# A macaron decoder trunk on eight cores: equal tile-major stages, half of an FFN's weights resident, all engines ordered by a list scheduler, input and output without transposes

## The chip, the cores and the metric

One Trainium2 chip, all eight NeuronCores. Two dies of four cores each: cores 0 to 3 and 4 to 7. Every core runs the same program on its own tokens; the cores do not talk to each other. The metric is the device time of one execution in microseconds (us), that of the slowest core.

A run can fall into a slow state: the cores of one die, or of both, show a lower granted TensorE clock, and their spans are longer (at 0.813 on one die, beside 0.996 to 0.998 in the fast runs). "Limiter" below is a name for whatever lowers the clock; what sets it off is not shown here. Every comparison below is either between fast runs or between dies on which the clock was left alone. Such a die is called undisturbed.

## The reference

Four layers; each is FFN, token mixer, FFN, each with a norm before and after it. Layers 0 and 2 mix with a gated convolution of width 3, layers 1 and 3 with causal pooling over 2, 4, 8 or 16 positions.

```python
def rmsnorm(x, g):
    y = x * lax.rsqrt(jnp.mean(x * x, axis=-1, keepdims=True) + EPS)
    return y * g
def swiglu(h, w_gate, w_up, w_down):
    return (silu(h @ w_gate) * (h @ w_up)) @ w_down
for i in range(4):                                   # D_MODEL 1024, D_FF 2816
    x = x + 0.5 * rmsnorm(swiglu(rmsnorm(x, g[0]), ...), g[1])
    h = rmsnorm(x, g[2])
    m = conv_mixer(h, ...) if i % 2 == 0 else pool_mixer(h, ...)
    x = x + rmsnorm(m, g[3])
    x = x + 0.5 * rmsnorm(swiglu(rmsnorm(x, g[4]), ...), g[5])
# ... outputs: y for 8 x 2048 prompt and 128 x 4 sample tokens, and the mixers' last rows
```

A core has 2,112 tokens. It does them in two passes of 1,056, each held on the chip as three tiles of 352 tokens. Activations lie feature-major: 8 chunks of 128 features on the partitions, tokens along the free dimension. All products are in bf16 with fp32 sums, so every matmul is 128 x 128 by 128 x 352.

## The kernel before

An operation list with hand-placed interleaving. Each engine is given its instructions in the order in which the program recorded them; semaphores are derived from the keys read and written. A tile's norms are recorded "deferred" and drained a few at a time between the matmuls of what follows.

```python
GROUPS = [5, 5, 4, 4, 4]        # FFN chunks of 128 hidden features; RING = 10 weight slots
def ffn(base_idx, finish, need, groups=GROUPS, prefix=1):
    units = [(gi, t) for t in range(NTILE) for gi in range(prefix)]
    units += [(gi, t) for gi in range(prefix, len(groups)) for t in range(NTILE)]
    # AB(ui): gate and up products of a unit, silu on ACT, product on DVE into gt
    # OUT(ui): for c in range(8): G matmuls into pso; ACT copies (gi == 0) or DVE adds into acc
    yield from AB(0)
    for ui in range(1, len(units)):
        yield from AB(ui)
        yield from OUT(ui - 1)          # finish(t) after the last group: the norms of tile t
# ...
def norm_stats(src, skey, t):           # ACT squares; 8 matmuls with ones sum them into pss (PSUM)
    # ...                               # ACT: Ln and Exp, in place in pss
def postnorm(l, n, t, half):            # DVE: acc = acc * gain * pss; x += acc on POOL (5) and DVE (3)
# ...
def pool_mixer(l, p, base_idx, finish, need):
    for t in range(NTILE):
        yield ("need", need(t))         # the pre-norm of the tile must be done
        for g in range(4):
            # per chunk: copy to a work tile, log2(w) shifted adds on POOL or DVE,
            # DVE: b2 = window / w - u; then 2 x 2 matmuls and a scale by DVE
        finish(t)
def boundary(p_store, p_load):          # between the passes, and at both ends
    # rows of 128 tokens: DMA to staging, 8 transposes on PE, ACT copies to xT; and back for y
```

Everything is recorded through one helper, so the profile names one line for it all; instructions are told apart by their tiles: psa are gate and up products, pso the down and mixer products, pss the sums of squares, b the bf16 squares (or mixer inputs), hreg the normed input, mt the mixers' scratch.

## Time and profile before

| | before |
|---|---|
| median of the first 3 runs | 5,863.55 us (5,766.8 to 6,026.48) |
| spans by core, profiled run | 5,696 to 5,888 us |
| PE busy, slowest core | 84% |
| fast runs on all chips used | 5,740 to 5,777 us, one of 5,804 us |

From the page of the profiled execution (the slowest core, core 1). First the span, then busy time and share of each engine, then the span in 40 slices: busy tenths of PE, and the clock granted to PE in tenths; then groups of instructions with their count, busy us, mean ns, and the engine's idle time just before them.

```profile
span 5887.5 us, 76218 instructions; the slowest of 8 cores (5696.2 to 5887.5 us)
...
PE 4964.6 (84%) x30208; PEld 3064.3 (52%) x30208; DVE 2439.9 (41%) x4900; ACT 1937.9 (33%) x3961; POOL 722.5 (12%) x1188
...
PE   6989999939988989975979789996698978989398
...
PEclk7777787858999999987989899997799989999599
...
L172 PE MATMUL psa<-hreg,ring 128*128 128x352 bf16 x18432 | 2991.1, 325 | 168.8 <-DMA ring<-wstream 94.5
...
L172 DVE TENSOR_TENSOR acc<-pso,acc 128x352 f32<-128x352 f32 x1536 | 791.7, 523 | 224.2 <-PE pso L172 179.2
...
L172 PE MATMUL pss<-b,ones_bf 128*128 128x352 bf16 x1152 | 273.1, 397 | 211.2 <-ACT b L172 81.5
```

PE is busy 84% and dips at four places, the four pool mixers (two layers in two passes). The 18,432 and 1,152 matmuls shown, 8,448 down products and two smaller groups of the page (960 and 768) make 29,760 of 352 columns, the work that no ordering removes.

Core 0 and core 2 of the same execution and die, in the same 200 us; the columns are the stretch, busy time and count of PE, weight loads, DVE, ACT and POOL, then the clock, the DMA share and GB/s:

```profile
600.00:800.00 200.00, 193.40 (x1051) 113.06 (x1049) 63.86 (x127) 44.27 (x82) 10.93 (x17) 0.80 0.26 48
```

```profile
600.00:800.00 200.00, 187.57 (x1240) 119.73 (x1238) 85.14 (x170) 61.05 (x119) 18.14 (x28) 1.00 0.43 80
```

Both are dense, but core 0 is granted 0.80 of the clock and gets 1,051 matmuls through, core 2 1.00 and 1,240. So core 1, which the page shows, is not the one to cost the change from. Core 4 was hardly limited and spans 5,696 us. Its waits of PE (us in total, times, longest):

```profile
PE pso L172 <- DVE b L172: 307.2, 44, 15.2
PE pso L172 <- DVE acc L172: 170.3, 116, 5.2
PE pss L172 <- ACT b L172: 86.4, 52, 4.5
...
PE psa L172 <- DMA ring<-wstream: 65.8, 25, 4.5
```

And five stretches of 20 us around its first pool mixer, columns as above:

```profile
1000.00:1020.00 20.00, 20.00 (x136) 13.12 (x135) 6.83 (x13) 9.69 (x18) 0.00 (x0) 1.00 0.31 63
1020.00:1040.00 20.00, 13.90 (x78) 7.23 (x76) 15.19 (x33) 13.07 (x29) 5.60 (x8) 0.91 0.00 0
1060.00:1080.00 20.00, 5.06 (x16) 2.07 (x16) 14.02 (x32) 5.84 (x16) 6.72 (x11) 0.50 0.68 141
...
1140.00:1160.00 20.00, 3.88 (x12) 1.48 (x12) 14.35 (x24) 6.67 (x20) 12.71 (x22) 0.50 0.00 0
1180.00:1200.00 20.00, 17.44 (x116) 11.08 (x115) 8.23 (x18) 15.72 (x29) 4.53 (x5) 1.00 0.00 1
```

136 matmul records per 20 us is full speed; in the middle of the mixer it is 12 to 26, and the clock is about 0.5 where PE idles: on core 4 it was 0.50 to 0.64 in 28 of the 32 such windows in which PE was busy for under 10 us, and 0.996 on the mean of the 134 in which PE never paused. DVE, ACT and POOL are not full either: it is one chain, each step waiting for the one before. Adding up what every 20 us window of core 4 falls short of 136 gives 1,175 us, of which about 480 at the four pool mixers.

### The profile page before, as it was taken

What the parts mean: (1) busy time and instruction counts of PE and PEld (TensorE: products, weight loads), DVE (VectorE), ACT (ScalarE), POOL (GpSimd) and SP (SyncE); (2) the same over time, 40 slices, a digit from 0 to 9 for tenths busy, and PEclk for the clock granted to TensorE, in tenths of its full rate; (3) what the DMA queues carried; (4) which work ended last, traced back from release to release, by engine and by line L of the source; (5) the groups of instructions that cost most, each with busy time, mean ns of one, the idle gap of its engine ahead of it and who ended that gap; (6) DMA issues with size and microseconds to landing.
All of it is one profiled execution on the core that took longest, in us unless ns stands there. A gap on an engine that the chain in (4) does not pass through costs nothing.

```text
span 5887.5 us, 76218 instructions; the slowest of 8 cores (5696.2 to 5887.5 us)
## 1 busy us (share of the span) xinstructions
PE 4964.6 (84%) x30208; PEld 3064.3 (52%) x30208; DVE 2439.9 (41%) x4900; ACT 1937.9 (33%) x3961; POOL 722.5 (12%) x1188
## 2 busy tenths in 40 slices
PE   6989999939988989975979789996698978989398
PEld 4545555615655556542646455553365644656155
DVE  1244333363434534355332543435434363343634
ACT  2133323134232433324141343423514135151342
POOL 0011001030101101013010110102201011010401
PEclk7777787858999999987989899997799989999599
DMA  4333222311333314230332332332032431414121
GB/s 85 70 55 60 38 54 45 74 34 30 68 70 70 66 38 81 49 70 17 70 97 49 70 66 40 79 60 60 8 74 45 92 65 29 90 29 92 34 49 47
DMA packets 64230, 341.58 MB, mean 58 GB/s; under 512 B 7390, under 2 KB 7646, under 8 KB 63840
## 3 DMA queue, kind: packets, MB, share of 16 engines
q0 software_dynamic: 57600, 314.60, 28.3%
q1 hardware_dynamic: 6272, 22.10, 1.1%
q8 instruction: 238, 3.90, 0.3%
q14 instruction: 120, 0.98, 0.1%
HBM read 641.66 MB, written 11.02 MB: 111 GB/s over the span
## 4 chain that ended last, share of the span: by engine, by line
PE 70%; DVE 10%; ACT 8%; DMA 5%; issue 4%; POOL 3%; ACTq 0%; POOLq 0%; SPq 0%; DVEq 0%
PE psa L172 44%; PE pso L172 23%; DVE acc L172 5%; PE pss L172 4%; DMA ring<-wstream 4%; ACT L172 3%; DVE hreg L172 2%; ACT b L172 2%; POOL xT L172 2%; DVE mt L172 1%; ACT pss L172 1%; POOL mt L172 1%; DVE b L172 1%; POOL ring L172 1%; ACT sa L172 1%
## 5 line engine op out<-in xcount | busy, mean ns | idle before, releaser
L172 PE MATMUL psa<-hreg,ring 128*128 128x352 bf16 x18432 | 2991.1, 325 | 168.8 <-DMA ring<-wstream 94.5
L172 PEld LDWEIGHTS psa<-hreg,ring 128*128 128x128 bf16 x18432 | 1860.5, 101 | 1244.7 <-DMA ring<-wstream 72.5
L172 DVE TENSOR_TENSOR gt<-psa,sa 128x352 bf16<-128x352 f32 x1056 | 553.7, 524 | 2452.2 <-PE psa L172 2059.2
L172 PE MATMUL pso<-gt,ring 128*128 128x352 bf16 x8448 | 1424.8, 327 | 147.0 <-DVE acc L172 140.2
L172 ACT ACTIVATE sa<-psa 128x352 f32<-128x352 f32 x1056 | 488.1, 464 | 2573.3 <-PE psa L172 2546.1
L172 PEld LDWEIGHTS pso<-gt,ring 128*128 128x128 bf16 x8448 | 842.1, 101 | 684.5 <-DVE acc L172 208.7
L172 DVE TENSOR_TENSOR acc<-pso,acc 128x352 f32<-128x352 f32 x1536 | 791.7, 523 | 224.2 <-PE pso L172 179.2
L172 POOL DMA_DIRECT2D ring<-wstream x400 | 214.0, 554 | 2881.6 <-PE pso L172 2834.0
L172 POOL TENSOR_TENSOR xT<-xT,acc 128x352 f32<-128x352 f32 x360 | 333.4, 953 | 1616.0 <-DVE acc L172 1505.4
L172 PE MATMUL pss<-b,ones_bf 128*128 128x352 bf16 x1152 | 273.1, 397 | 211.2 <-ACT b L172 81.5
L172 PE MATMUL pso<-b,ring 128*128 128x352 bf16 x960 | 186.9, 356 | 311.4 <-DVE b L172 307.0
L172 ACT ACT_TABLE_LOAD x297 | 381.1, 1283 | 140.9 <-PE psa L172 135.6
L172 DVE SCALAR_TENSOR_TENSOR hreg<-xT,params_sb,pss 128x352 bf16<-128x352 f32 x480 | 245.3, 575 | 240.3 <-ACT pss L172 240.3
L172 ACT ACTIVATE b<-xT 128x352 bf16<-128x352 f32 x576 | 259.1, 490 | 164.5 <-POOL xT L172 116.9
L172 PEld LDWEIGHTS pss<-b,ones_bf 128*128 128x128 bf16 x1152 | 129.7, 118 | 338.0 <-issue 72.4
L172 PEld LDWEIGHTS pso<-b,ring 128*128 128x128 bf16 x960 | 98.0, 107 | 396.1 <-DVE b L172 316.3
L172 ACT ACTIVATE acc<-pso 128x352 f32<-128x352 f32 x480 | 222.7, 464 | 220.2 <-PE pso L172 219.4
L172 ACT ACTIVATE b<-acc 128x352 bf16<-128x352 f32 x576 | 238.9, 487 | 15.2 <-DVE acc L172 15.2
L172 DVE SCALAR_TENSOR_TENSOR acc<-acc,params_h,pss 128x352 f32<-128x352 f32 x384 | 200.2, 575 | 78.4 <-ACT pss L172 78.4
L172 DVE SCALAR_TENSOR_TENSOR mt<-mt,params_sb 128x352 f32<-128x352 f32 (+2 forms) x256 | 126.4, 494 | 88.8 <-ACT mt L172 84.3
L172 ACT ACTIVATE pss<-pss,epst 128x352 f32<-128x352 f32 x144 | 76.0, 528 | 247.0 <-PE pss L172 246.5
L172 DVE SCALAR_TENSOR_TENSOR acc<-acc,params_sb,pss 128x352 f32<-128x352 f32 x192 | 101.0, 575 | 115.8 <-ACT pss L172 115.8
(56 smaller groups left out, 1369.1 us busy)
## 6 DMA issues: line engine op xcount, KB each, us to landing
ring<-wstream POOLq DMA_DIRECT2D x400, 768.0 KB, 12.6
mt<-x_in SPq DMA_DIRECT2D x16, 512.0 KB, 7.7
y_o<-mt SPq DMA_DIRECT2D x16, 512.0 KB, 3.2
stg<-spool SPq DMA_DIRECT2D x4, 480.0 KB
ps_s<-spool SPq DMA_DIRECT2D x4, 352.0 KB
ps_s<-stg SPq DMA_DIRECT2D x32, 16.0 KB
mt<-x_in SPq DMA_DIRECT2D x2, 128.0 KB, 3.1
stg<-sconv SPq DMA_DIRECT2D x4, 64.0 KB
```

The costliest lines, as they stand in the source:

```text
L172: ins = attr(*a, **k)
```

## The change

The intent: keep PE fed through every norm and mixer. Stages go tile by tile with equal work; an FFN runs in two halves of 11 chunks whose weights stay resident for all three tiles, so that two whole tiles of matmuls (78 us) lie between a tile's last product and its next need; a list scheduler with durations for every operation places all instructions of all engines at build time; tokens come in and go out feature-major, so PE transposes nothing (the host rearranges them before and after, outside the device time). The diff replaces most of the file; its core:

```diff
-GROUPS = [5, 5, 4, 4, 4]
-RING = 10
+GRP = 11
+RU = 24                     # weight ring, units of 1,024 columns: 11 gate/up pairs and one spare
+LAT = {"pe": 0.22, "act": 0.10, "dve": 0.10, "pool": 0.12, "sp": 0.05}
+MM = 0.1490
+def c_act(n, sb=False): return 0.172 + 0.000833 * n + (0.022 if sb else 0.0)
+def c_dve(n): return 0.150 + 0.001042 * n
 # ...
+class Sched:
+    def op(self, eng, fns, cost, reads=(), writes=(), vts=(), prio=0, margin=0.0, dma=None, ...):
+        # records dependencies; vts are PSUM banks, assigned when the schedule is made
+    def run(self):
+        # event-driven list scheduling: at each step the engine and operation that can start
+        # first, ties by (prio, program order); 7 banks for products, 1 for the sums of squares
+                else:
+                    t = o.end + LAT[e] + q.margin     # when a successor on another engine may start
 # ...
-        P.op("act", ... Exp, in place in pss)          # post-norm products read pss in PSUM
+        S.op("act", [Ln in place, lambda a: a.activation(out=rr[b][:], in_=B(v)[:, 0:TS], func=AF.Exp, scale=-0.5)], ...)
+            S.op("pe", f, 4 * MM, reads=[... ("sq", b, c) ...], vts=[v], prio=P_STAT, margin=0.6)
 # ...
+    def ffn(f, finish):
+        for g in range(2):
+            slots = [load_units(wab[f, g * GRP + jj], 2) for jj in range(GRP)]
+            # ... 8 loads of down weights, wdn[dc], 11 chunks each
+            for t in range(NTILE):
+                ffn_tile(g, t, slots, finish)
 # ...
+            def fin1(t, ...):
+                postnorm(l, 1, t, True)
+                prenorm(l, 2, t, to_u=not conv)
+                if not conv:
+                    pool_tile(l, p, t, fin2)            # a tile's whole pool mixer, norms included
 # ...  pool windows of 8 and 16 by one DVE scan each; conv and pool squares straight from PSUM
-    def boundary(p_store, p_load): ...                  # transposes and staging
+    def load_x(p, t): ...                               # DMA to x[t] as it lies, and store_y back
```

## The prediction

> **What bounds it now.** TensorE: the page gives PE 84% of the span, the chain of waits is 70% PE. The groups hold 29,760 real matmuls of 352 columns (18,432 + 8,448 + 960 + 768 + 1,152; 448 more are transposes). In undisturbed 20 us windows a core completes 136, 147 ns each: 29,760 x 0.147 = 4,370 us, a floor at full clock. Core 4, hardly limited, spans 5,696 us: some 1,300 us is not dense matmul.
>
> Where that lies (20 us windows of core 4, PE's waits):
> - four pool mixers, each 130-150 us with 8-29 matmuls per 20 us at clock 0.5: about 120 us lost each, 480 us. The waits name DVE b (307 us), DVE acc, ACT b: one chain of norm, windows, small matmul, norm, norm.
> - first 80 us: about 50 lost; pass boundary and end (transposes, staging): about 80.
> - conv mixers, FFN seams, ring waits (66-95 us), each 3-18 us per window: the rest, about 600.
>
> **What the change does.** FFN and stats matmuls and weight bytes stay. It removes the transposes, their evictions and fences, and the pass boundary's serial store and load. Groups of 11 instead of 4-5 cut the accumulate adds (1,536 x 523 ns) to 384: 600 us less DVE, off the critical path. One FFN half x one tile is 264 matmuls, 39 us, so a tile's norm chain has the other two tiles' 78 us as cover. I estimate a post+pre-norm chain at 26 us (16 squares of 0.49, two Ln/Exp with 1.28 us table loads, 16 products of 0.575, 8 adds): hidden. Pool: about 80 us, and ACT needs about 44 us per 39 us tile: nearly hidden, 15 us left each. Weights per half are 8.65 MB; the first windows moved 150-215 GB/s, so 40-58 us of 118: hidden.
>
> **Fast state (estimate).** 4,370 + start 30 + end 25 + pools 4 x 15 + imperfect static order 1.5% (65) = 4,550 us. DVE and ACT about 40% busy, PE 96-97%.
>
> **Limiter.** Cores 0 and 1 ran at 0.81 from the start to about 1,150 us, cores 2 and 3 from about 4,450 to 5,560; others stayed at 1.00 in the same dense code. [...] dense dies ran at 1.00, and pairs were hit. An episode cost 150-200 us. [...] Held throughout it would be 29,760 x 0.177 + 200 = 5,470 us.
>
> **Prediction.** 4,700 us for the median run (best near 4,550), range 4,500 to 5,250. Faster by over 2%: 0.97, within 2%: 0.01, slower: 0.02.
>
> **Right if:** pool stages no longer dip in the slices of PE; dense windows hold 136 matmuls per 20 us at 1.00, 113 where limited; DVE b vanishes from PE's waits; table loads stay near 290; weight loads aren't among PE's waits beyond the first 100 us.
>
> **Wrong if:** the limiter holds throughout; all cores' weight bursts, concentrated in the third tile, exceed what HBM gives and PE waits at each half; weight issues on POOL, blocked on buffers, hold up residual adds; ACT or DVE saturates around the pool mixers; or the fixed order, made with modelled times, stalls in-order engines.

The fast state came to 4,550 us, and a run held at the lower clock throughout to 5,470 us. The 0.177 us in the latter is 20 us over 113 matmuls, which is the count at 0.81 (112 or 113 in the windows of cores 0 and 1 from 960 to 1,000 us, against 136 at 1.00). The point of 4,700 us lies 150 us above the fast state; that the median run would be a slow one was the author's estimate, not shown.

## The result, and the profile after

| | before | after |
|---|---|---|
| median of 6 runs | 5,820.38 us (5,750.89 to 6,289.14) | 4,808.14 us (4,533.64 to 5,433.13) |
| fast runs | 5,751 to 5,777 us | 4,533.64 and 4,534.30 us |
| ratio of the fast runs | | 0.7857 (95%: 0.7812 to 0.7902) |
| PE busy, profiled run | 84% | 98% |

A ratio is the mean time of one kernel's fast runs over that of the other's of the same rounds, so not quite the ratio of the medians quoted. Only two of the six new runs were fast; the other four had one die or both at a lower clock, from 4,708 us (0.955) to 5,433 us (0.813).

The page after, of a fast execution, the same lines as before (core 6):

```profile
span 4532.7 us, 70376 instructions; the slowest of 8 cores (4528.3 to 4532.7 us)
...
PE 4459.6 (98%) x29760; PEld 2911.6 (64%) x29760; DVE 1926.4 (42%) x3581; ACT 1832.7 (40%) x3527; POOL 824.2 (18%) x1329
...
PE   7999999999999999999999999999999999999998
...
PEclk9999999999999999999999999999999999999999
...
L350 PE MATMUL ps<-h,ring 128*128 128x352 bf16 x19200 | 2924.4, 313 | 0.0
...
L350 DVE TENSOR_TENSOR acc<-ps,acc 128x352 f32<-128x352 f32 x384 | 200.7, 523 | 454.3 <-PE ps L350 453.8
...
L350 PE MATMUL ps<-sq,ones_bf 128*128 128x352 bf16 x1152 | 223.0, 318 | 58.4 <-ACT sq L350 39.9
```

The four dips are gone from the slices. VectorE's adds fell from 1,536 to 384. PE on core 4 before was idle for 908 us and busy for 4,788 (at a mean clock of 0.914); here it is idle for 73 and busy for 4,460 (at 0.996). So most of the gain is idle time, and some 330 us are busy time, with the clock at 0.996 instead of 0.914 and the 448 transposes gone. These are all the waits of PE:

```profile
PE ps L350 <- ACT sq L350: 39.9, 23, 11.4
PE ps L350 <- ACT rr L350: 18.4, 13, 3.1
PE ps L350 <- DVE gt L350: 0.8, 2, 0.6
```

59 us in all, none of them for weights. Windows around the first pool mixer, and one long dense stretch:

```profile
840.00:860.00 20.00, 18.90 (x127) 12.21 (x126) 11.54 (x27) 13.09 (x27) 2.61 (x4) 1.00 0.16 27
880.00:900.00 20.00, 18.50 (x123) 11.75 (x122) 16.38 (x27) 10.17 (x19) 8.77 (x14) 1.00 1.04 163
920.00:940.00 20.00, 16.35 (x97) 9.68 (x95) 16.62 (x33) 16.08 (x29) 3.81 (x5) 0.91 0.00 1
940.00:960.00 20.00, 20.00 (x136) 13.11 (x134) 14.68 (x34) 10.76 (x25) 5.79 (x9) 1.00 0.08 32
1200.00:1800.00 600.00, 599.76 (x4020) 393.02 (x4019) 250.10 (x472) 234.48 (x452) 106.87 (x190) 1.00 0.46 74
```

97 to 127 records where there had been 12 to 26. By the same count core 6 falls short of full speed by 79 us, 38 of them at the pools and nearly all the rest in the first 60 us; the last 13 us, after its last matmul, come on top. The long stretch also corrects a reading: 4,020 records in 600 us are 149.3 ns each, or 149.2 by the 599.76 us for which PE was busy. A 20 us window counts the matmuls that stick out of either end too, so 136 records are about 134 matmuls.

### The profile page after: what moved, and what is told of

The parts are those of the page before. It is cut to its first block, busy times and chain, and to the rows that moved or that the text cites. A ratio compares the mean times of both kernels' runs of the same rounds, so it can differ in the third digit from the quotient of the medians.

```text
span 4532.7 us, 70376 instructions; the slowest of 8 cores (4528.3 to 4532.7 us)
## 1 busy us (share of the span) xinstructions
PE 4459.6 (98%) x29760; PEld 2911.6 (64%) x29760; DVE 1926.4 (42%) x3581; ACT 1832.7 (40%) x3527; POOL 824.2 (18%) x1329
## 4 chain that ended last, share of the span: by engine, by line
PE 93%; DVE 4%; ACT 2%; DMA 1%; issue 0%; SPq 0%; DVEq 0%
PE ps L350 93%; DVE acc L350 2%; DMA x<-x_in 1%; ACT sq L350 1%; DVE x L350 1%; DVE gt L350 0%; ACT L350 0%; DVE h L350 0%; ACT ps L350 0%; ACT sa L350 0%; ACT rr L350 0%; DVE scr L350 0%; ACT acc L350 0%; SPq L350 0%; DVEq L368 0%
## 5 line engine op out<-in xcount | busy, mean ns | idle before, releaser
L350 PE MATMUL ps<-h,ring 128*128 128x352 bf16 x19200 | 2924.4, 313 | 0.0
L350 PEld LDWEIGHTS ps<-h,ring 128*128 128x128 bf16 x19200 | 1881.4, 98 | 990.7 <-DVE h L350 0.5
L350 PE MATMUL ps<-gt,wdn 128*128 128x352 bf16 x9216 | 1406.6, 313 | 1.1 <-DVE gt L350 0.8
L350 DVE TENSOR_TENSOR gt<-ps,sa 128x352 bf16<-128x352 f32 x1056 | 550.2, 522 | 1929.7 <-PE ps L350 1893.1
L350 PEld LDWEIGHTS ps<-gt,wdn 128*128 128x128 bf16 x9216 | 901.2, 98 | 475.6 <-DVE gt L350 2.9
L350 ACT ACTIVATE sa<-ps 128x352 f32<-128x352 f32 x1152 | 531.8, 462 | 1387.6 <-PE ps L350 1333.1
L350 POOL TENSOR_TENSOR x<-x,acc 128x352 f32<-128x352 f32 x288 | 323.6, 1146 | 979.9 <-DVE acc L350 979.2
L350 ACT ACTIVATE sq<-x 128x352 bf16<-128x352 f32 x576 | 271.5, 494 | 190.5 <-DVE x L350 83.4
L350 DVE SCALAR_TENSOR_TENSOR acc<-acc,params_h,rr 128x352 f32<-128x352 f32 x384 | 312.1, 861 | 28.5 <-ACT rr L350 28.5
L350 DVE SCALAR_TENSOR_TENSOR h<-x,params_sb,rr 128x352 bf16<-128x352 f32 x480 | 254.6, 578 | 51.3 <-ACT rr L350 50.8
```

Of the source, the lines that this page charges most:

```text
L350: ins = attr(*a, **k)
```

## The experiments

The theory after the result: in the fast state the gain is PE's idle time at chains, put under the matmuls of other tiles. Rivals were that resident weights, fewer VectorE adds or the missing transposes carry it, and that the scheduler's durations hardly matter. All kernels below gave correct results. In what follows the undisturbed die's span is quoted; the new kernel's is 4,531 us, the kernel before has about 5,740 us. The first four runs were on one chip, the others on two more; the new kernel was run again on one of these as a control, and gave the same span.

### Program order on three engines

The scheduler stays, but PE, DVE and ACT must take their operations in the order of the program.

```diff
+        if eng in ("pe", "act", "dve"):
+            prev = self.prev_on.get(eng)
+            if prev is not None and prev.idx not in deps:
+                prev.succ.append(o)          # order only, no semaphore
+                o.ndep += 1
+            self.prev_on[eng] = o
```

> The new kernel, but TensorE, VectorE and ScalarE take their instructions in the order in which the program lists them; weight loads and the other work of POOL and SP stay list-scheduled. Theory A (the gain is that other tiles' matmuls are put into the time of a tile's norm chain, which the list scheduler does): every chain stands open again. 72 tiles at seams x about 15 us (3 us before each sum of squares, 12 us between the two norms) plus some 45 us for each of 12 pool tiles: a span of 5,900 to 6,600 us in the fast state, PE busy 65 to 75%, waits of PE for ACT and DVE instead of near none. Rival B (resident half weights, fewer adds and feature-major input and output carry the gain, and the order only polishes it): under 4,900 us.

Measured: all four runs had a slow die; undisturbed dies took 5,743 to 5,764 us, so at least 1,212 us more than the new kernel. Waits of PE on core 4 of the less disturbed die:

```profile
PE ps L357 <- ACT sq L357: 732.3, 216, 22.5
PE ps L357 <- DVE h L357: 173.6, 48, 8.9
```

The size was missed (5,900 or more was expected); the direction and the waits are as theory A had them. Rival B falls: with every structural part of the change in place and only the order undone, the whole gain is gone, to within some 25 us. (Program order is harsher than the order before, which was interleaved by hand; so this does not say that the structure is worth nothing, but that it gains nothing in this order.)

### Groups of 5, 5, 4, 4, 4 again

```diff
+GS = [5, 5, 4, 4, 4]
-        for g in range(2):
-            slots = [load_units(wab[f, g * GRP + jj], 2) for jj in range(GRP)]
+        for g in range(len(GS)):
+            slots = [load_units(wab[f, G0[g] + jj], 2) for jj in range(GS[g])]
# gate and up products in program order, and after the buffer they lead to is free: without it the
# scheduler stops, all PSUM banks held by products whose successors wait for a bank
```

With two groups of 11 these added order rules leave PE's order nearly as it is: the scheduler, run without a chip, gives about 40 lines of difference in 3,648 entries, and 4,506 us instead of 4,497 by its own durations. What they cost with the small groups was not separated, since the scheduler stops without the first rule.

> The new kernel with FFN groups of 5, 5, 4, 4, 4 chunks as before, instead of two halves of 11; list scheduler kept. Theory A (what counts is the cover that the last and first group give a tile's chain: two tiles of a group of 4 are 2 x 14.3 = 28.6 us, not 78): ordinary chains of about 26 us just fit, pool chains of about 80 us do not. About 80 to 100 us lost at each of four pool mixers, a few us at the other seams: 4,850 to 5,050 us in the fast state, dips of PE at the pools only. Rival B (the list scheduler does it with any group size): under 4,600 us. Rival C (the saved VectorE adds carry it, 1,536 instead of 384): loss spread evenly over the FFN stretches, not at the pools.

Measured: 4,918.16 and 4,917.17 us, both fast, 4,893 us on die 0: 362 us more. Page of that run and waits of core 0:

```profile
PE 4578.6 (93%) x29760; PEld 2933.6 (60%) x29760; DVE 2528.6 (51%) x4733; ACT 1724.1 (35%) x3453; POOL 1047.4 (21%) x1713
...
PE   7999999789999999969989999996999999999698
```

```profile
PE ps L358 <- ACT sq L358: 128.7, 43, 11.6
PE ps L358 <- DVE h L358: 84.6, 35, 9.3
```

The dips are back at the pools: by the count of windows about 285 of 439 us short of full speed lie there, against 38 of 79 in the new kernel, 62 us more at each pool mixer. Rival B falls, and rival C too: VectorE is busy 51% instead of 42%, but the loss does not follow its work. The remaining 110 us or so sit at the other seams, more than "a few us": probably an ordinary chain does not quite fit in 28.6 us. So, the added order rules apart, the resident half pays as cover, not as saved adds.

### Gates at the pool mixers, then at every seam

```diff
+    def gate():              # written when the last tile has left the stage
+        S.op("dve", lambda v: v.memset(gtile[:], 0.0), 0.1, reads=[("x", NTILE - 1, c) ...], writes=["gate"])
+            ffn(2 * l, fin1)
+            if not conv:
+                gate()
+                for t in range(NTILE):
+                    prenorm(l, 2, t, to_u=True, gated=True)    # its squares read "gate"
+                    pool_tile(l, p, t, fin2)
```

> The new kernel, but no tile enters the pool mixer before the last tile has left the FFN in front of it (four gates). Theory A (the pool's long chain is hidden because tile 0 may run it while TensorE works on tiles 1 and 2): at each gate the chain of tile 0 from the norm through the windows to the next norm, about 55 us, stands open, less the 12 us lost there now: 4,700 to 4,830 us in the fast state. Rival (the pool mixer itself has become cheap through scans and through copies from PSUM, so that its place matters little): under 4,600 us.

Measured: 4,720 us on die 0 (4,762.66 us for the run; the other die was at 0.966). 189 us more, 47 us a gate. Waits of PE there:

```profile
PE ps L350 <- ACT sq L350: 119.6, 34, 12.0
PE ps L350 <- DVE h L350: 67.9, 24, 5.8
```

Theory A, with its size; the cheaper mixer alone would have left under 70 us.

> As the one with four gates, with gates at all seams within a pass, 18 in all, so that no tile begins the next stage's norm before the last tile has left the stage before. Theory A: 14 more gates of about 20 to 26 us each on top of the four at the pools, 280 to 360 us more than that run: about 5,050 to 5,200 us in the fast state. Rival (the ordinary seams are hidden by something else, such as weight prefetch): less than 100 us more than the run with four gates.

Measured: 5,037 to 5,040 us on die 0 (5,059.82 us for the fast run), 318 us more than with four gates, 23 us for each of the 14 others. As expected for theory A. ("Every seam" leaves out the one behind each pool mixer and the one between the passes, which have no gate.) The chains that lie hidden are therefore about 47 us at a pool and 23 us elsewhere. (The last tile's post-norm is within the gate, so these are upper values of what stands open.)

### Wrong durations for the scheduler

```diff
-        o.cost = cost
+        o.cost = cost if eng in ("pe", "sp") or dma else 0.5 * cost
-LAT = {"pe": 0.22, "act": 0.10, "dve": 0.10, "pool": 0.12, "sp": 0.05}
+LAT = {"pe": 0.0, "act": 0.0, "dve": 0.0, "pool": 0.0, "sp": 0.0}
-                cost += 1.35          # table load
+                cost += 0.65
```

> The new kernel, its list scheduler fed with wrong durations: everything outside TensorE and the DMA costs half of what the trace shows, and semaphore latencies count as zero. Theory A (the order is robust, because 78 us of cover is three times an ordinary chain, so durations need not be right): the span grows by less than 1%, 4,530 to 4,580 us in the fast state, the growth at the pools. Rival (the calibrated costs are what makes the order fit, and a wrong model stalls the in-order engines): over 4,650 us.

Measured: 5,067 to 5,079 us on undisturbed dies, 5,088.81 us in the one fast run: 537 us more. My theory failed here and the rival held. PE's waits, core 5:

```profile
PE ps L350 <- ACT sq L350: 334.3, 128, 11.3
PE ps L350 <- DVE h L350: 66.9, 39, 3.8
```

128 waits for squares, 2.6 us each. Cover does not help an instruction that stands too early in a fixed order: at each of these waits PE stood still at a sum of squares whose squares were late, and the gate products behind it waited too. In the trace what followed the sums went on without a pause after 123 of the 128 waits, so it had been ready. That became the next theory.

### The same wrong durations, sums of squares held back

```diff
-                 prio=P_STAT, margin=0.6)
+                 prio=P_STAT, margin=6.0)      # and the same for the pool's products
```

> The run with halved costs took 5,068 us on an undisturbed die, so the earlier theory of a robust order fell. This kernel has the same wrong costs, but the scheduler keeps every small matmul that sums squares (and the pool's matmuls) 6 us behind what feeds it, instead of 0.6 us. Theory A' (with wrong costs those matmuls stand in TensorE's fixed order before their squares exist, and TensorE, which takes matmuls in order, stands still at each; cover is of no use if the matmul is placed too early): PE's wait for ACT sq falls from 334 us to under 80 us, and the span to 4,600 to 4,750 us on an undisturbed die. Rival (everything is misplaced: gates, evictions, table switches, bank choice): the span stays above 4,900 us.

Measured: 4,801 to 4,814 us on the better die, between the two expectations. Waits of PE, core 0:

```profile
PE ps L350 <- DVE gt L350: 146.0, 49, 8.0
PE ps L350 <- ACT rr L350: 74.6, 23, 7.5
PE ps L350 <- ACT sq L350: 16.4, 7, 8.3
```

The wait for squares fell from 334 to 16 us, as the theory says, and half of the loss with it (266 of 537 us). The other half stays, now as waits of down products for gt and of sums for the bank that Exp still reads (rr), so the rival is half right: those are misplaced as well.

### The old kernel with feature-major input and output

```diff
-    def boundary(p_store, p_load): ...                   # staging, transposes, copies
+    def boundary(p_store, p_load):
+        for t in range(NTILE):
+            # store x of tile t as it lies; load the next pass's tile t over it
-        transposed_out(lambda c: csamp[:, c, :], 16, ...)
+        feature_out("cs_s", csamp[:].rearrange("p a b -> p (a b)"), cs_s[j, p], [("csamp",)])
# likewise the loads of histories and the other state outputs; everything else as before
```

> The kernel before with only the feature-major input and output of the change: no transposes on TensorE, no staging, states loaded and stored directly; everything else as before. Theory A (this part is worth the first 80 us, the pass boundary, the end and the fences around state transposes, and nothing else): 80 to 170 us less than before, so about 5,590 to 5,680 us in the fast state. Rival B (the transposes' fences and staging also held up the pool and conv mixers, so most of their idle time goes too): more than 300 us less. Rival C (the chains that start each stage take the same time anyway): less than 50 us.

Measured: fast runs 5,674.02 and 5,668.70 us beside 5,748 to 5,757 us of the kernel before on that chip (one more at 5,804): 81 us less between the means without that one, 94 with it, the low end of theory A. DVE b stays the longest of PE's waits there:

```profile
PE pso L172 <- DVE b L172: 314.1, 48, 14.6
```

So input and output without transposes are worth 7 or 8% of the gain by themselves.

### Fewer matmuls for the sums of squares

```diff
+        S.op("dve", ... sq[:, 0:4] = sq[:, 0:4] + sq[:, 4:8] ...)
+        S.op("dve", ... sq[:, 0:2] = sq[:, 0:2] + sq[:, 2:4] ...)
-            8 matmuls with ones
+            2 matmuls with ones
# in short; the sums are lambdas as elsewhere
```

> The new kernel, with VectorE adding the eight chunks of squares of each norm to two (bf16, two wide instructions), so that TensorE sums 2 instead of 8: 864 fewer matmuls of 149 ns, 129 us. Theory A (TensorE at 98% is the only limit left in the fast state, other engines have room): the span falls by 115 to 130 us, to about 4,405 to 4,420 us, 2.5 to 2.9%. Rival (the norm chains are already at the edge, and 1 to 2 us more VectorE work in each pushes them out from under the cover): less than 60 us gained, with more waits of PE at the pools.

Measured: three fast runs at 4,461.59 to 4,465.85 us, ratio to before 0.7743 (0.7689 to 0.7796). Die 1 took 4,429 to 4,437 us, 100 us less than the new kernel; die 0 took 4,458 to 4,464 us in the same runs at a clock of 0.986 instead of 0.995. Most of the 129 us, but not all. Waits of PE, core 5:

```profile
PE ps L350 <- DVE sq L350: 40.9, 12, 18.5
```

The one of 18.5 us is at the start, where the new kernel waits as well (29 us for squares in the first 60 us). What is lost lies at the pool mixers: by the count of windows core 5 is 60 us short of full speed there, the new kernel 38.

### All residual adds on VectorE

```diff
-            eng = "pool" if c < 4 else "dve"
+            eng = "dve"
```

> The new kernel with all residual adds on VectorE, none on POOL. The products of the post-norm, whose operands all lie in SBUF since the change, averaged 861 ns there with single ones up to 3.3 us, against 575 ns and at most 582 ns before, when one operand lay in PSUM. Theory [...]: without the adds on POOL the mean falls back to 575 to 600 ns outside the pool mixers. Rival (the operand in SBUF is slow by itself): it stays over 800 ns. The span changes by less than 1% either way, since VectorE is 42% busy.

(What is tested is whether the long products go when POOL's adds do.)

The products of the post-norm, in the three kernels: count, then shortest, median and longest ns. Before (core 4, pss in PSUM):

```profile
L172 DVE SCALAR_TENSOR_TENSOR acc<-acc,params_h,pss x384: 567/574/582, 307.6 to 5680.1; 128x352 f32<-128x352 f32 x192
```

After (core 6, rr in SBUF):

```profile
L350 DVE SCALAR_TENSOR_TENSOR acc<-acc,params_h,rr x384: 569/585/3253, 203.8 to 4526.9; 128x352 f32<-128x352 f32 x192
```

After, without adds on POOL (core 5):

```profile
L350 DVE SCALAR_TENSOR_TENSOR acc<-acc,params_h,rr x384: 574/580/586, 202.6 to 4494.6; 128x352 f32<-128x352 f32 x192
```

The operand in SBUF is not slow by itself (median 585 ns); but 170 of the 384 took over 0.7 us, up to 3.25 us, each with a residual add of POOL beside it. The 167 with none beside them took at most 587 ns, and without the residual adds on POOL the longest is 586 ns. With one operand in PSUM, in the kernel before, 270 of the 384 had such an add beside them, and the longest of these took 579 ns. So the product is longer here where all its operands lie in SBUF and POOL adds at the same time. The longest one has three residual adds of POOL (0.93 to 0.94 us each) and two of its weight-DMA issues beside it. What delays it is not shown. Moving rr from PSUM to SBUF, a side effect of the change, had brought this on these products; VectorE's own residual adds met it before already (up to 3.40 us on core 4). The span is 4,501 to 4,503 us on die 1, 30 us less. By the count of windows 12 us are now lost at the pool mixers instead of 38, so VectorE mattered there (it had been busy for 16.6 of 20 us in the window at 920 us). By the scheduler's own durations, which know of no such lengthening, the edit gains nothing (4,499 us against 4,497); so the lengthening is the likely cause, though POOL's adds are also longer than VectorE's (1,146 ns on the mean against 512 in the new kernel).

### Three edits together, and the version that beats both

All residual adds and the partial sums on VectorE, and the first weight loads held until the first input tile has landed:

```diff
+            first = 2 <= st["ld"] < GRP
-                 0.55, writes=[...], dma=f"ring{...}", ...)
+                 0.55, reads=[("x", 0, c) ...] if first else [], writes=[...], dma=f"ring{...}", ...)
+        # gate and up products in program order (the scheduler stopped without it)
```

> The new kernel unchanged, as a control on this chip: 4,531 us, within 5 us, on a die that the limiter leaves alone.

> The new kernel with three edits together: squares summed to two chunks on VectorE, all residual adds on VectorE, and the first weight loads behind the first tile of the input (with the gate and up products kept in program order). Theory (TensorE is the only limit, the parts add): 4,531 less 101 (measured for the first), less 30 (measured for the second), less about 15 for the start (PE begins at 37 us now) = about 4,385 us on an undisturbed die, 4,370 to 4,420. Rival (VectorE becomes the limit around the pool mixers, where both edits add to its work): above 4,430 us, with dips at the pools.

Measured on that chip: the control 4,527 to 4,533 us on die 0 in five of its six runs. The three edits gave 4,486 to 4,492 us on die 0 at a clock of 0.988, 100 us more than the sum promised. (One of nine runs took 8,260 us with clocks of 0.56 to 0.75; nothing here explains it.) Waits of PE:

```profile
PE ps L356 <- DVE h L356: 60.7, 15, 7.9
PE ps L356 <- DVE sq L356: 33.3, 5, 17.9
PE ps L356 <- DMA ring<-wab: 12.9, 4, 11.7
```

Of the 61 us for h 53 are at the pools, but of the 33 for partial sums 24 are at the start, and so are 12 of those for the weights that were held back. By the count of windows 91 us are lost at the pools (12 with the adds on VectorE alone) and 50 in the first 60 us (35 in the new kernel). So the span and the dips are as the rival had them, and the start edit lost time. That VectorE's load alone did it is not shown: gate and up products in program order, which the start edit needed, are another cause that no run separates. The scheduler, run without a chip, puts this kernel at 4,476 us, at 4,454 without the start edit, at 4,435 without that order too, and the last version, below, at 4,415: by its durations each has a part. So the last version keeps the adds on VectorE, leaves the start alone, and uses partial sums except in the four norms around each pool mixer:

```diff
+        if presum:               # False around the pool mixers
+            # two adds on DVE, 2 matmuls
+        else:
+            # 8 matmuls as in the new kernel
-            eng = "pool" if c < 4 else "dve"
+            eng = "dve"
```

> The new kernel with all residual adds on VectorE, and squares summed to two chunks on VectorE except in the four norms around each pool mixer (96 of 144 norms: 576 fewer matmuls of 149 ns, 86 us); the start as in the new kernel. Theory (TensorE is the only limit outside the pool mixers, VectorE is near its limit at them, which is why the three edits together did not add): 4,501 us measured with the adds alone, less 86 = about 4,415 us on a die that the limiter leaves alone, 4,405 to 4,430, without DVE sq among PE's waits at the pools. Rival (the two edits disturb each other anywhere): above 4,450 us. In the fast state against the kernel before: a ratio of about 0.768.

Measured: 4,416 to 4,419 us on undisturbed dies; two fast runs of eight, 4,420.45 and 4,420.56 us, beside 5,740 to 5,776 us before (three fast runs) on that chip, a ratio of 0.768 between the means. Against the new kernel's 4,534 us on another chip that is 2.5% less. Page and waits of core 0:

```profile
span 4418.0 us, 69513 instructions; the slowest of 8 cores (4417.2 to 4942.4 us)
...
PE 4360.6 (99%) x29184; PEld 2855.4 (65%) x29184; DVE 2023.8 (46%) x4061; ACT 1810.5 (41%) x3531; POOL 502.7 (11%) x1041
```

```profile
PE ps L350 <- DVE sq L350: 20.9, 2, 18.2
PE ps L350 <- DVE h L350: 12.2, 2, 7.9
```

Of the waits for partial sums, one of 18 us is most, and it is at the start; at the pools there is none, as expected. 29,184 matmuls of 149.2 ns are 4,354 us of the 4,418, so what remains is the start, the end and the clock.

## Why the prediction was right

The measured median, 4,808 us, lies inside the stated range, 108 us over the point; the fast state, put at 4,550 us, measured 4,534 us. The second is the test of the mechanism. How near the median came is partly luck, since it hangs on how many of six runs were slow (four). Point by point:

- **The bound.** Right in kind: TensorE stays the limit, and the floor decides. The floor itself was read 1.6% too low: "136 matmuls per 20 us, 147 ns each" counted records that cross a window's ends. 149.2 ns makes it 4,440 us, not 4,370.
- **The static order** was charged 65 us. It cost next to nothing outside the pools; the two errors cancelled. The count of windows for core 6 shows 38 us at the pools, not 60, and 54 us for start and end, as against 55. 4,440 + 38 + 54 is the span, 4,532 us.
- **The pool mixers**, 120 us each before, now about 10 instead of the predicted 15. That they would be hidden by the other two tiles is what the runs with small groups and with gates show.
- **Off the critical path.** The saved VectorE adds were said to be worth nothing by themselves, and the small groups bear this out: the loss sat at the seams.
- **Weights.** Said to be hidden; PE has no wait for DMA at all.
- **Chains.** Put at 26 us and, at the pools, at "about 80 us". A gate cost 23 and 47 us. The first agrees. The second cannot be read from a gate alone, since a gate opens only the part up to the first tile's next product.
- **Signs.** No dips at the pools, DVE b gone, and 136 records per 20 us at 1.00: right; a limited stretch holds 112 or 113 at 0.81 (last version, core 6; as on cores 0 and 1 of the kernel before). Table loads fell to 235 instead of staying near 290, probably because the scheduler ran some norms back to back (not tested).
- **"Wrong if the fixed order, made with modelled times, stalls in-order engines."** It did not, but the danger was real: with halved durations and no latencies the same kernel loses 537 of its 1,209 us. I had taken the opposite for granted in the expectation of that run.
- **The limiter.** Right that the median would lie above the fast state for this reason; the new runs that were slow spread from 4,648 to 5,433 us. Held throughout at 0.813, a die took 5,430 us, against the predicted 5,470. On the chain of the kernel before, 80 gate and up products at 0.81 took 14.44 us, 180.5 ns each (core 1, at 976 us). Dense work alone did not lower the clock: in the profiled fast run all eight cores had PE busy for 98% at 0.996 or 0.997. Whether episodes became more frequent is open. A slow die was seen in 13 of 24 cases for the new kernel and 19 of 56 for the kernel before, but on different chips; on the one chip that ran both in the same rounds, in 7 of 12 and 5 of 14. There the new kernel never had a fast run, since one die was at 0.966 to 0.976 at best, while the kernel before ran on that die at its usual 0.91 or so in six of seven runs. Why is not shown; no run here tests it.

What was shown and what was argued: that the order carries the gain and that cover makes it possible is shown by runs that undo each. What sets the limiter off is not shown. What share VectorE's load had in the failed sum of three edits is argued only.

## What to carry to other kernels

When the busiest engine waits on chains of short steps, the gain needs two things at once: enough independent work between a tile's last product and its next need, and an order that puts it there; undoing the first here (smaller groups) gave back 362 of 1,209 us, undoing the second (program order, harsher than the hand-placed one) all of it. A static order is as good as its durations: take them from a trace, and hold small dependent instructions back by a margin on an in-order engine, since one that stands too early stops all that is ready behind it (2.6 us at each of 128 here). After such a change look for the operands that moved between memories (861 ns instead of 575 for the post-norm's products here) and for the engine that is nearly full at one stage only (VectorE, 16.6 of 20 us at a pool mixer); edits that gain singly there need not add.
